# One decoder layer on one core: earlier loads of x pieces, output blocks in pairs, joined loads of keys, queries and factors

## The chip, the core and the metric

The kernel runs on one core of a Trainium2 chip. A core has a matrix engine (PE, with its weight loads listed as PEld), a vector engine (DVE), a scalar engine (ACT), GpSimd (POOL) and a sync engine (SP), which in this kernel issues every DMA. The transfers themselves are carried out by 16 DMA engines. The metric is the device time of one execution in microseconds; lower is better. The median of three runs of the kernel before is 1200.78 us (1198.64 to 1202.95).

## The reference, cut to what matters

One layer for 2048 prompt positions and 8 sample tokens, everything in float32:

```python
h = x @ w_in                       # queries, keys, values, gates of mixers A and B
for d in (1, 4, 16):               # mixer A, 8 heads: banded attention at three strides
    parts.append(band_partial(dilate(qa, d), dilate(ka, d), dilate(va, d)))
oa = merge(parts)                  # weighted by the softmax denominators
ob = merge([band_partial(qb, kb, vb)], sink)   # mixer B, 8 query heads on 2 key heads
mix = concat(oa * silu(ga), ob * silu(gb))
y = layer_norm(ALPHA * x + mix @ w_o)
```

The sample tokens go through the same layer against cached keys and values.

## The kernel before

Every float32 product is made of three products of halves: an operand is split into a rounded part and the rest (`split`: ACT copies, DVE or POOL subtracts), and the matmuls take high x high, high x low and low x high.

**Stages.** First the projections of A's keys and queries and of all keys, then the values (L527). From about 376 us on runs the attention stage, the loop at L1121 of 64 steps. A pair is two heads of one mixer. The four pairs of A have three jobs each (strides 16, 4 and 1), the four pairs of B one job; a job is four steps. A step makes the scores of one group (`scores`, L823), its weights on DVE and ACT (L831, L834), turns the weights of the step before on PE (`turn`, L853) and multiplies those of the step before that with the values (`values`, L874). In four slots of each step `advance` lets the generator `others` put work of a second stream between: the remaining projections (`stream`), then the first part of the output projection (`out_weights`). After the loop the last part computes the rest of the output projection and the layer norm (L1174).

**Order.** Inside the attention stage the order on every engine is the order in which the program is written (a manual schedule). SP issues its DMAs in that order too, and a DMA that waits holds up all that stand behind it on SP. Eight semaphores take turns for the DMAs, so a DMA also waits until the one eight places before it on SP has landed.

**The second stream (L603 to L641).** It makes three passes over x, whose split form lies in DRAM in eight chunks of 256 tokens (the last has 264), each in four pieces `gx` of 512 KB. The passes have 4, 4 and 3 column blocks of the weights (`FIRST`, then G1 to G4, then G5 to G7); one block on one chunk is 24 matmuls `pg` (L629). There are two sets of four buffers for the pieces; the pieces of the next chunk are loaded by `piece` (L576) while the present one is used.

**Keys, queries and factors.** `load_k` and `load_q` (L893, L901) fetch the keys and queries of the next pair, head by head, in halves of 1024 positions. After the last job of a pair in B, `merge_b` (L944) makes the factors of both heads, turns them on PE (`pst`, L963), writes them to DRAM (`fd`) and reads them back, spread over the 64 partitions of each head, into `F` (L976 to L981), with which the output `oT` is multiplied (L990). For A this is `merge_a` (L1001), whose loads of `F` stay as they are.

**Output blocks ahead.** The output has 17 blocks: 16 of 128 tokens and the sample tokens. For the first four, `out_weights` (L722) computes the part of the sum over the 8 row blocks of the weights (0 to 3 are A, 4 to 7 are B) that is ready: `gated` (L707) loads the gates and merged outputs of one block, `hh` and `hl` are its split form, and `out_products` (L667) does the matmuls `po`. `gated` takes 6 row blocks instead of 4 for an even block if more than one pair of B is merged by then. The last part adds what is missing (`mixed`, L648).

Of the kernel before, what the change touches and what calls it, by code (L numbers as in the profile page):

```python
# [11 lines left out]
F32 = mybir.dt.float32  # L12
F32R = mybir.dt.float32r
AF = mybir.ActivationFunctionType
OP = mybir.AluOpType
AX = mybir.AxisListType

D = 1024
# [22 lines left out]
FIRST = ["QB0", "QB1", "QB2", "G0"]  # L41
PT = (1, 4, 7, 10, 13)
RAW = 4
AHEAD = 4


def dram(t, off, ap):
# [4 lines left out]
def hymba_step(ctx, tc, xt, xs, xr, wq, wv, wo, tab, msk, ident, diag, sinks, lng, lnb,  # L52
# [513 lines left out]
    def stream(passes):  # L566

        with tc.tile_pool(name="gw", bufs=1, side="right", reuse_waits="tile") as gw, \
                tc.tile_pool(name="gx", bufs=2, side="right", reuse_waits="tile") as gx, \
                tc.tile_pool(name="go", bufs=2, side="right", reuse_waits="tile") as go, ExitStack() as fourth:  # L570
            g4 = fourth.enter_context(tc.tile_pool(name="g4", bufs=1, side="right", reuse_waits="tile"))
            news = None

            place = count(4)

            def piece(c, k0):  # L576
                c0 = 256 * c
                n = TOK - c0 if c == 7 else 256
                i = next(place) % 8
                t = (kept if i < 4 else gx).tile([128, 4 * XC], F32R, name="gx", tag="p%d" % i, bufs=1)[:, :4 * n]  # L580
                dma(t.bitcast(F32), xd[c, k0, :, :4 * n])
                t = t.rearrange("p (a k n) -> p a k n", a=2, k=2)
                return t[:, 0], t[:, 1]

            def weights(i, name):
                if i < 2:
                    t = kept.tile([128, 2, 8, 128], F32R, name="gw%d" % i, tag="w%d" % i)
                    hl = t[:, 0], t[:, 1]
                else:
                    hl = [(gw if i < 3 else g4).tile([128, 8, 128], F32R, name="gw%d%s" % (i, a)) for a in "hl"]  # L590
                ws[name].open(hl)

            ws = dict(zip(passes[0], resident_w))
            def first_wo(i):
                t = kept.tile([128, 2, 8, 128], F32R, name="wo%d" % i, tag="w%d" % i)
                wo_parts[4 + i].open((t[:, 0], t[:, 1]))

            nxt = X5
            yield 0
            for i in (2, 3):  # L600
                ws[passes[0][i]] = Parts(wq[TILES.index(passes[0][i])])
                weights(i, passes[0][i])
            for pi, names in enumerate(passes):  # L603
                more = passes[pi + 1] if pi + 1 < len(passes) else []
                if not more:
                    fourth.close()
                    sp = fourth.enter_context(tc.tile_pool(name="spb", bufs=1, side="right", reuse_waits="tile"))
                    sk = fourth.enter_context(tc.tile_pool(name="skb", bufs=1, side="right", reuse_waits="tile"))
                    news = sample("b", sp, sk)
                route = list(range(8))[::1 if pi % 2 else -1]  # L610
                for c, c2 in zip(route, route[1:] + [None]):
                    c0 = 256 * c
                    n = TOK - c0 if c == 7 else 256
                    x, nxt = nxt, []
                    if c2 is None:
                        for name in more:
                            ws[name] = Parts(wq[TILES.index(name)])
                        if not more:
                            head.append(gated(0))
                            wo_parts.update((i, Parts(wo[:, i].rearrange("p (a b) -> p a b", b=128))) for i in (4, 5))  # L620
                    for i, name in enumerate(names):
                        p = ps.tile([128, 512], F32, name="pg", tag="mm", bufs=2)
                        wh, wl = ws[name]
                        for kt in range(8):
                            if c2 is not None and kt % 2 == 0 and i == 1:
                                nxt.append(piece(c2, len(nxt)))
                            xh, xl = x[kt // 2]
                            for e, (a, b) in enumerate(((wh, xh), (wh, xl), (wl, xh))):
                                T.matmul(p[:, :n], a[:, kt, :], b[:, kt % 2, :n], start=kt + e == 0, stop=kt == 7 and e == 2)  # L629
                                yield n / 2.4  # L630
                        EMIT[name[0]](go, XC, p[:, :n], name, c0, n)
                        if name[0] == "Q":
                            queries.append(name)
                        if news:
                            next(news, None)
                        if c2 is None:
                            if not more and i < 2:
                                soon(lambda i=i: first_wo(i), 1)
                            for e in range(i, len(more) if name == names[-1] else min(i + 1, len(more))):
                                soon(lambda e=e, name=more[e]: weights(e, name), 1)  # L640
                nxt = x  # L641
            for _ in news:
                pass
# [60 lines left out]

    head = []

    def gated(tb):  # L707

        n = 6 if len(merged) > 1 and tb % 2 == 0 else 4
        cols = slice(tb * 128, tb * 128 + 128)  # L710
        t, g = [kept.tile([128, 6, 128], F32, name="h" + a, tag="p%d" % i)[:, :n] for i, a in enumerate("tg")]
        dma(g, gs[0:n, :, cols].rearrange("k p t -> p k t"))
        dma(t, ms[0:n, :, cols].rearrange("k p t -> p k t"))
        return t, g

    def late_wo(kt):
# [5 lines left out]
    def out_weights():  # L722
        wO = wscope.enter_context(tc.tile_pool(name="wO", bufs=1, side="right", reuse_waits="tile"))
        for kt in (6, 7):
            out_parts(kt, [wO.tile([128, 8, 128], F32R, name="wo%d%s" % (kt, a)) for a in "hl"])
            yield None
            yield None
        oh = wscope.enter_context(tc.tile_pool(name="oh", bufs=1, side="right", reuse_waits="tile"))
        xs_ = [oh.tile([128, D], F32, name="xh%d" % tb) for tb in range(AHEAD)]
        nxt = head[0]  # L730
        first.clear()
        for tb, x in enumerate(xs_):
            t, g = nxt
            dma(x, xr[tb * 128:tb * 128 + 128])
            for _ in range(3 if tb else 1):
                yield None
            n = t.shape[1]
            h, l = [oh.tile([128, 4, 128], F32R, name="h" + a, tag="h" + a) if tb % 2 else kept.tile([128, 6, 128], F32R, name="h" + a, tag="p%d" % (i + 2))
                    for i, a in enumerate("hl")]
            V.tensor_mul(t, t, g)  # L740
            split(h[:, :n], l[:, :n], t, V)
            yield None
            if tb + 1 < AHEAD:
                nxt = gated(tb + 1)
            for nh in range(2):
                p = ps.tile([128, 512], F32, name="po", tag="mm", bufs=2)
                yield from out_products(p, {kt: (h[:, kt], l[:, kt]) for kt in range(n)}, nh, True, True)
                xx = x[:, nh * 512:nh * 512 + 512]
                V.scalar_tensor_tensor(xx, xx, ALPHA, p, op0=OP.mult, op1=OP.add)
            first[tb] = x, n  # L750

    MI = {16: 0, 4: 1, 1: 2}
    PB, PA = (1,), (16, 4, 1)
# [139 lines left out]
    def load_k(p):  # L893
        p.k = kp.tile([128, SEQ], F32, name="k")
        for c in range(2):
            for h in range(2):
                cc = slice(1024 * c, 1024 * c + 1024)
                dma(p.k[64 * h:64 * h + 64, cc], ks[:, p.pair // 2 if p.isb else 2 + 2 * p.pair + h, cc])
            yield

    def load_q(p):  # L901
        p.q = kp.tile([128, SEQ], F32, name="q")
        for c in range(2):
            for h in range(2):
                cc = slice(1024 * c, 1024 * c + 1024)
                dma(p.q[64 * h:64 * h + 64, cc], (qb if p.isb else qa)[:, 2 * p.pair + h, cc])
            yield

    dr2 = ctx.enter_context(tc.tile_pool(name="dr2", bufs=2, space=bass.MemoryType.DRAM))
# [34 lines left out]
    def merge_b(job):  # L944
# [12 lines left out]
        V.tensor_add(dn, dn, w[:, 1])  # L957
        V.reciprocal(dn, dn)
        V.scalar_tensor_tensor(w[:, 0], w[:, 0], 0.5, dn, op0=OP.mult, op1=OP.mult)
        while where[0] < 3:  # L960
            yield
        pst = ps.tile([128, 512], F32, name="pst", tag="pt", bufs=2)
# [13 lines left out]
        def fetch(c):  # L976
            F = at.tile([128, 768], F32, name="F", bufs=2)
            n = min(768, SEQ - 768 * c)
            for a in range(2):
                dma(F[a * 64:a * 64 + 64, :n], dram(fd, a * SEQ + c * 768, [[0, 64], [1, n]]))  # L980
            Fs.append(F[:, :n])  # L981

        fetch(0)
# [355 lines left out]
```

## Time and profile before

| | before |
|---|---|
| profiled execution, time | 1196.65 us |
| profiled execution, span | 1194.9 us |
| median of 3 runs | 1200.78 us |
| DMA issues by SP | 1011 |
| matmuls in the attention stage and the rest, up to the sample block | 376 to 1026 us |
| last part, from the sample block on | 1026 to 1195 us |

The profile's page gives the busy time of each engine, the span in slices, the DMA queues and the costliest groups of instructions; further views give the busy time and the DMA share by stretches of time ("windows"), who waited for whom ("waits"), and the instructions in order of time ("timeline"). "DMA share" is the mean busy share of the 16 DMA engines. PEclk is the share of full speed at which the matrix engine's clock was granted.

### The profile page before, as it was taken

Reading aid. Unit: us, or ns where it says so; the run is one execution under the profiler, and the core shown is the slowest. Engines: PE = TensorE matmul, PEld = TensorE weight load, DVE = VectorE, ACT = ScalarE, POOL = GpSimd, SP = SyncE. Lnnn points to the kernel's source line nnn. Section 1 sums busy time; section 2 is a strip of 40 time slices with the busy share of each in tenths; the row PEclk is TensorE's granted clock in tenths of the full one; section 3 lists DMA queues with packets and bytes.
Section 4 is the critical chain, followed back from the end, with each engine's and each line's share of the span. In section 5 each row is a group of like instructions: output and inputs, shape, how many; then the busy total and the mean of one; then the engine's idle time right before and its main releaser. Section 6 shows DMA issues by size and latency. Waiting matters only on the chain.

```text
span 1194.9 us, 23402 instructions
## 1 busy us (share of the span) xinstructions
PE 1138.3 (95%) x8614; PEld 1004.4 (84%) x8614; DVE 540.0 (45%) x1787; ACT 438.1 (37%) x1417; POOL 360.0 (30%) x470
## 2 busy tenths in 40 slices
PE   8999999999989999999998999998999997999997
PEld 7899999988978988997887879887878875688885
DVE  6532000011002455565565546554656664675534
ACT  3200011111102556565565545554555451232211
POOL 2243010220002200034704401462254534275532
PEclk9999999999999999999999999998999998999998
DMA  8845888375495575458677856866897967555531
GB/s 275 267 132 160 255 269 281 106 227 177 150 316 172 181 185 164 133 129 216 194 207 166 210 174 158 208 157 201 198 237 190 305 191 214 172 190 181 179 107 70
DMA packets 206066, 230.14 MB, mean 193 GB/s; under 512 B 34640, under 2 KB 174576, under 8 KB 205568
## 3 DMA queue, kind: packets, MB, share of 16 engines
q1 hardware_dynamic: 205952, 228.66, 66.3%
q8 instruction: 67, 1.10, 0.4%
q14 instruction: 47, 0.39, 0.1%
HBM read 158.52 MB, written 70.07 MB: 191 GB/s over the span
## 4 chain that ended last, share of the span: by engine, by line
PE 68%; DMA 17%; POOL 4%; issue 3%; DVE 3%; ACT 3%; SPq 2%; POOLq 0%; DVEq 0%; ACTq 0%
PE po L672 13%; PE pg L629 12%; PE pv L527 7%; PE ps_s L823 6%; PE ps_o L874 6%; DMA F<-fd 5%; PE ps_pt L853 5%; PE ppt L152 5%; PE pmm L152 5%; PE ps L152 5%; PE po L152 3%; DMA gx<-xd 3%; DMA wvf<-in_wv 1%; ACT pe L834 1%; DMA fd<-wts 1%
## 5 line engine op out<-in xcount | busy, mean ns | idle before, releaser
L834 ACT ACTIVATE pe<-sm,st 128x256 f32<-128x256 f32 (+1 forms) x512 | 236.6, 464 | 218.0 <-DVE st L831 217.4
L831 DVE CUSTOM_DVE_ANT_0 sm<-ps_s,mk 128x256 f32<-128x256 f32 (+1 forms) x512 | 180.2, 375 | 193.0 <-PE ps_s L823 129.4
L629 PE MATMUL pg<-gx,gw 128*128 128x256 f32 (+1 forms) x1104 | 169.0, 295 | 18.5 <-DMA gx<-xd 13.6
L629 PEld LDWEIGHTS pg<-gx,gw 128*128 128x128 f32 x1104 | 143.0, 192 | 21.4 <-DMA gx<-xd 15.3
L853 PE MATMUL ps_pt<-idt,pe 128*128 128x128 f32 x848 | 134.5, 279 | 1.9 <-DVE pT L859 1.4
L1050 POOL TENSOR_TENSOR oT<-oT,F 128x256 f32<-128x256 f32 x32 | 23.7, 742 | 339.5 <-DMA F<-fd 302.2
L859 DVE COPY pT<-ps_pt 128x512 f32<-128x512 f32 x176 | 120.6, 685 | 5.5 <-PE ps_pt L853 5.0
L853 PEld LDWEIGHTS ps_pt<-idt,pe 128*128 128x128 f32 x848 | 96.1, 141 | 15.5 <-issue 8.8
L874 PE MATMUL ps_o<-pT,v 128*64 128x128 f32 (+1 forms) x1120 | 107.1, 335 | 0.0
L874 PEld LDWEIGHTS ps_o<-pT,v 128*64 128x64 f32 x1120 | 70.2, 137 | 40.1 <-issue 16.6
L834 ACT ACTIVATION_READ_ACCUMULATOR pe<-sm,st 128x1 f32 x512 | 96.5, 188 | 0.0
L823 PE MATMUL ps_s<-k,qo 64*128 64x256 f32 (+1 forms) x768 | 94.4, 387 | 0.0
L823 PEld LDWEIGHTS ps_s<-k,qo 64*128 64x128 f32 x768 | 68.5, 193 | 13.2 <-issue 1.7
L629 PE MATMUL pg<-gx,gw2h 128*128 128x256 f32 (+1 forms) x368 | 75.7, 293 | 1.8 <-ACT spe L406 1.8
L527 PE MATMUL pv<-wvh,xl 128*128 128x384 f32 (+1 forms) x224 | 69.9, 312 | 0.0
L527 PE MATMUL pv<-wvh,xh 128*128 128x384 f32 (+1 forms) x224 | 69.8, 312 | 0.0
L527 PE MATMUL pv<-wvl,xh 128*128 128x384 f32 (+1 forms) x224 | 69.7, 311 | 0.0
L629 PEld LDWEIGHTS pg<-gx,gw2h 128*128 128x128 f32 x368 | 58.6, 191 | 2.1 <-ACT spe L406 2.1
L672 PE MATMUL po<-wl,mho 128*128 128x512 f32 x192 | 59.8, 393 | 0.0
L539 ACT ACTIVATE vf<-pv 128x384 f32<-128x384 f32 (+1 forms) x32 | 14.0, 437 | 113.0 <-PE pv L527 63.7
L629 PE MATMUL pg<-gx,gw2l 128*128 128x256 f32 (+1 forms) x184 | 54.3, 295 | 0.2 <-POOL gw2l L138 0.2
L260 POOL TENSOR_TENSOR wl<-w,wh 128x512 fp32r<-128x512 f32 x18 | 24.5, 1374 | 83.9 <-DVE wh L259 62.9
(262 smaller groups left out, 2474.7 us busy)
## 6 DMA issues: line engine op xcount, KB each, us to landing
gx<-xd SPq DMA_DIRECT2D x80, 512.0 KB
F<-fd SPq DMA_DIRECT2D x80, 192.0 KB
gs<-th SPq DMA_DIRECT2D x64, 128.0 KB
v<-vs SPq DMA_DIRECT2D x28, 256.0 KB
xd<-xh SPq DMA_DIRECT2D x12, 512.0 KB
xd<-xl SPq DMA_DIRECT2D x12, 512.0 KB
kc<-in_kca SPq DMA_DIRECT2D x8, 768.0 KB
vc<-in_vca SPq DMA_DIRECT2D x6, 1024.0 KB
```

The costliest lines, as they stand in the source:

```text
L152: T.matmul(p[:, :n], a[:, kt, :], b, start=k == 0, stop=k == 23)
L260: (V if between else G).tensor_sub(l[:, k0:k0 + 4], w, h[:, k0:k0 + 4].bitcast(F32))
L527: T.matmul(p[:, :w], l, r[:, kt, :w], start=k == 0, stop=k == 23)
L629: T.matmul(p[:, :n], a[:, kt, :], b[:, kt % 2, :n], start=kt + e == 0, stop=kt == 7 and e == 2)
L672: T.matmul(p, a, b[:, nh * 4:nh * 4 + 4].rearrange("p a b -> p (a b)"), start=first and k == 0, stop=last and k == end)
L823: T.matmul(s[:, h, n % 4, :w], self.Q[g][r, n % 4 * 128:n % 4 * 128 + 128], self.keys(n)[r], start=True, stop=True)
L831: V.tensor_tensor_reduce(sm[:, :w], self.s[:, h, n % 4, :w], mk[:, MI[self.d], 256 - w:], -0.125, 3.0e38, op0=OP.add, op1=OP.min, accum_out=m)
L834: S.activation(p[:, :w], sm[:, :w], AF.Exp, scale=-1.0, bias=m, accum_out=den)
L853: T.transpose(pt[:, h, j], self.P[h, n][:, a:a + 128], idt)
L859: V.tensor_copy(t, pt)
L874: T.matmul(o[64 * h:64 * h + 64, a:a + 128 * len(ns)], v[:, cv, kv:kv + 64], t[:, h, j:j + len(ns)].rearrange("p a b -> p (a b)"), start=n ...
L1050: G.tensor_mul(m, m, F[:, 0])
```

## The change

Four edits, here in the diff cut to its core:

```diff
-                            if c2 is not None and kt % 2 == 0 and i == 1:
+                            if c2 is not None and (i, kt) in ((0, 2), (0, 4), (0, 6), (1, 0)):
                                 nxt.append(piece(c2, len(nxt)))
...
-    def gated(tb):
-        n = 6 if len(merged) > 1 and tb % 2 == 0 else 4
-        cols = slice(tb * 128, tb * 128 + 128)
-        t, g = [kept.tile([128, 6, 128], F32, name="h" + a, tag="p%d" % i)[:, :n] for i, a in enumerate("tg")]
+    def gated(j):
+        cols = slice(j * 256, j * 256 + 256)
+        t, g = [kept.tile([128, 4, 256], F32, name="h" + a, tag="p%d" % i) for i, a in enumerate("tg")]
...
-        for tb, x in enumerate(xs_):
+        for j in range(2):
             t, g = nxt
+            xs_ = [(oh if tb < 3 else kp).tile([128, D], F32, name="xh%d" % tb, ...) for tb in (2 * j, 2 * j + 1)]
+            for tb, x in zip((2 * j, 2 * j + 1), xs_):
+                dma(x, xr[tb * 128:tb * 128 + 128])
...
     def load_k(p):
         for c in range(2):
-            for h in range(2):
-                cc = slice(1024 * c, 1024 * c + 1024)
-                dma(p.k[64 * h:64 * h + 64, cc], ks[:, p.pair // 2 if p.isb else 2 + 2 * p.pair + h, cc])
+            h = p.pair // 2 if p.isb else 2 + 2 * p.pair
+            dma(p.k[:, 1024 * c:1024 * c + 1024], dram(ks, h * TOK + 1024 * c, [[0 if p.isb else TOK, 2], [10 * TOK, 64], [1, 1024]]))
     def load_q(p):
...
+            dma(p.q[:, 1024 * c:1024 * c + 1024], dram(qb if p.isb else qa, 2 * p.pair * TOK + 1024 * c, [[TOK, 2], [8 * TOK, 64], [1, 1024]]))
...
         V.scalar_tensor_tensor(w[:, 0], w[:, 0], 0.5, dn, op0=OP.mult, op1=OP.mult)
+        yield
         while where[0] < 3:
             yield
         pst = ps.tile([128, 512], F32, name="pst", tag="pt", bufs=2)
...
-            for a in range(2):
-                dma(F[a * 64:a * 64 + 64, :n], dram(fd, a * SEQ + c * 768, [[0, 64], [1, n]]))
+            dma(F[:, :n], dram(fd, c * 768, [[SEQ, 2], [0, 64], [1, n]]))
```

A joined load has 128 partitions on the chip's side, and on the DRAM side a pattern of three dimensions whose outermost has 2 entries, the heads. The output blocks ahead are done two at a time, with 4 row blocks for all four.

The rows below, and those in the two fences after them, are the program's order on one engine, without any time. On SP, in the attention stage while the third pair's keys are fetched (`k<-ks`), among the factors of A (`F<-fd`), pieces of x (`gx`), merged outputs (`ms`) and gates (`gs`), before:

```order
L1038 DMA F<-fd_5260 64x3x256 x2
L898 DMA k<-ks 64x1024 x2
L581 DMA gx<-xd 128x1024 x2
L1058 DMA ms<-oT_5524 128x256
L898 DMA k<-ks 64x1024 x2
L581 DMA gx<-xd 128x1024
L1038 DMA F<-fd_5260 64x3x256 x2
L581 DMA gx<-xd 128x1024
```

The same place after the change:

```order
L580 DMA gx<-xd 128x1024
L1036 DMA F<-fd_5258 64x3x256 x2
L580 DMA gx<-xd 128x1024
L1056 DMA ms<-oT_5522 128x256
L580 DMA gx<-xd 128x1024
L174 DMA gs<-th 128x256
L1036 DMA F<-fd_5258 64x3x256 x2
L898 DMA k<-ks 128x1x1024
L580 DMA gx<-xd 128x1024
L1056 DMA ms<-oT_5522 128x256
L898 DMA k<-ks 128x1x1024
L1036 DMA F<-fd_5258 64x3x256 x2
```

Three of the four pieces now stand ahead of the keys, the fourth between the two halves; each half of the keys is one DMA of 128 partitions instead of two of 64.

On PE, around the last but one turn of factors (`pst`), between turns of weights (`ps_pt`) and gate matmuls (`pg`), before:

```order
L853 MATMUL ps_pt<-idt,pe 128x128 x4
L629 MATMUL pg<-gx,gw_9611 128x256 x8
L963 MATMUL pst<-idt,wts 32x128
L823 MATMUL ps_s<-k,qo 128x256 x8
L874 MATMUL ps_o<-pT,v 64x256 x6
```

And after:

```order
L854 MATMUL ps_pt<-idt,pe 128x128 x4
L628 MATMUL pg<-gx,gw_9595 128x256 x8
L962 MATMUL pst<-idt,wts 32x128
L824 MATMUL ps_s<-k,qo 128x256 x8
L875 MATMUL ps_o<-pT,v 64x256 x6
```

Nothing moved here: the chain of factors takes one slot more on paper, but it waits for the step's last slot in either version. This holds for all four turns of factors.

On SP, where the factors of B's second pair are read back, before (`hg`, `ht` are the loads of `gated`):

```order
L968 DMA fd_10612<-stT 16x16x8 x2
L581 DMA gx<-xd 128x1024 x3
L980 DMA F<-fd_10612 64x768 x4
L581 DMA gx<-xd 128x1024
L175 DMA gs<-th 128x256 x2
L980 DMA F<-fd_10612 64x512 x2
L712 DMA hg<-gs 128x4x128
L713 DMA ht<-ms 128x4x128
```

And after:

```order
L580 DMA gx<-xd 128x1024 x3
L174 DMA gs<-th 128x256
L967 DMA fd_10596<-stT 16x16x8 x2
L580 DMA gx<-xd 128x1024
L978 DMA F<-fd_10596 128x1x768 x2
L174 DMA gs<-th 128x256 x2
L978 DMA F<-fd_10596 128x1x512
L710 DMA hg<-gs 128x4x256
L711 DMA ht<-ms 128x4x256
```

Six loads of factors became three, and the first loads for the output blocks are twice as large.

More of the change, by code (lines that the diff above doesn't have):

```diff
@@ L43 @@
 RAW = 4
-AHEAD = 4
 def dram(t, off, ap):
@@ L705, in hymba_step @@
     head = []
-    def gated(tb):
-        n = 6 if len(merged) > 1 and tb % 2 == 0 else 4
-        cols = slice(tb * 128, tb * 128 + 128)
-        t, g = [kept.tile([128, 6, 128], F32, name="h" + a, tag="p%d" % i)[:, :n] for i, a in enumerate("tg")]
-        dma(g, gs[0:n, :, cols].rearrange("k p t -> p k t"))
-        dma(t, ms[0:n, :, cols].rearrange("k p t -> p k t"))
+    def gated(j):
+        cols = slice(j * 256, j * 256 + 256)
+        t, g = [kept.tile([128, 4, 256], F32, name="h" + a, tag="p%d" % i) for i, a in enumerate("tg")]
+        dma(g, gs[0:4, :, cols].rearrange("k p t -> p k t"))
+        dma(t, ms[0:4, :, cols].rearrange("k p t -> p k t"))
         return t, g
@@ L728, in out_weights @@
         oh = wscope.enter_context(tc.tile_pool(name="oh", bufs=1, side="right", reuse_waits="tile"))
-        xs_ = [oh.tile([128, D], F32, name="xh%d" % tb) for tb in range(AHEAD)]
         nxt = head[0]
         first.clear()
-        for tb, x in enumerate(xs_):
+        for j in range(2):
             t, g = nxt
-            dma(x, xr[tb * 128:tb * 128 + 128])
-            for _ in range(3 if tb else 1):
+            xs_ = [(oh if tb < 3 else kp).tile([128, D], F32, name="xh%d" % tb, **(dict(tag="k", bufs=2) if tb == 3 else {}))
+                   for tb in (2 * j, 2 * j + 1)]
+            for tb, x in zip((2 * j, 2 * j + 1), xs_):
+                dma(x, xr[tb * 128:tb * 128 + 128])
+            for _ in range(1 if j == 0 else 2):
                 yield None
-            n = t.shape[1]
-            h, l = [oh.tile([128, 4, 128], F32R, name="h" + a, tag="h" + a) if tb % 2 else kept.tile([128, 6, 128], F32R, name="h" + a, tag="p%d" % (i + 2))
+            h, l = [oh.tile([128, 4, 256], F32R, name="h" + a) if j else kept.tile([128, 4, 256], F32R, name="h" + a, tag="p%d" % (i + 2))
                     for i, a in enumerate("hl")]
             V.tensor_mul(t, t, g)
-            split(h[:, :n], l[:, :n], t, V)
+            split(h, l, t, V)
             yield None
[L743 to L750, printed above, removed]
+            if j == 0:
+                nxt = gated(1)
+            for tb, x in zip((2 * j, 2 * j + 1), xs_):
+                cols = slice(tb % 2 * 128, tb % 2 * 128 + 128)
+                for nh in range(2):
+                    p = ps.tile([128, 512], F32, name="po", tag="mm", bufs=2)
+                    yield from out_products(p, {kt: (h[:, kt, cols], l[:, kt, cols]) for kt in range(4)}, nh, True, True)
+                    xx = x[:, nh * 512:nh * 512 + 512]
+                    V.scalar_tensor_tensor(xx, xx, ALPHA, p, op0=OP.mult, op1=OP.add)
+                first[tb] = x, 4
     MI = {16: 0, 4: 1, 1: 2}
@@ L903, in load_q @@
         for c in range(2):
-            for h in range(2):
-                cc = slice(1024 * c, 1024 * c + 1024)
-                dma(p.q[64 * h:64 * h + 64, cc], (qb if p.isb else qa)[:, 2 * p.pair + h, cc])
+            dma(p.q[:, 1024 * c:1024 * c + 1024], dram(qb if p.isb else qa, 2 * p.pair * TOK + 1024 * c, [[TOK, 2], [8 * TOK, 64], [1, 1024]]))
             yield
```

## The prediction

> **What bounds the kernel now.** I read the page's busy times first, then the chain, then the stages.
>
> ```profile
> PE 1138.3 (95%) x8614; PEld 1004.4 (84%) x8614; DVE 540.0 (45%) x1787; ACT 438.1 (37%) x1417; POOL 360.0 (30%) x470
> ```
>
> ```profile
> PE 68%; DMA 17%; POOL 4%; issue 3%; DVE 3%; ACT 3%; SPq 2%; POOLq 0%; DVEq 0%; ACTq 0%
> ```
>
> The first line gives each engine's busy time (us, share of the span, instructions), the second the chain that ended last, by engine. PE is busy 95% of the span, so no wait that is left is large; the second thing on the chain is the transfers. What they could do is seen by stages. The windows are the four pairs of A, and then the rest of the attention stage with B's pairs and the start of what follows:
>
> ```profile
> core 0: us, PE busy (x), PEclk, DMA share, GB/s
> 376.00:484.00 108.00, 105.18 (x951) 0.98 0.61 183
> 484.00:592.00 108.00, 106.33 (x965) 0.98 0.65 162
> 592.00:702.00 110.00, 102.22 (x890) 0.95 0.79 212
> 702.00:819.00 117.00, 112.72 (x1017) 1.00 0.64 154
> 819.00:855.00 36.00, 33.46 (x268) 0.91 0.81 223
> 855.00:895.00 40.00, 36.64 (x328) 0.96 0.94 224
> 895.00:933.00 38.00, 35.16 (x306) 1.00 0.80 207
> 933.00:969.00 36.00, 33.55 (x298) 1.00 0.77 253
> 969.00:1006.00 37.00, 29.95 (x202) 0.93 0.73 226
> ```
>
> In each row the numbers behind the stretch are its length, the busy time of PE, the granted clock, the mean busy share of the 16 DMA engines and the bytes moved. PE sets the pace everywhere, but from 819 us on the DMA engines are at 0.73 to 0.94. A change that spreads the same bytes less evenly has room for little there.
>
> The waits that the change aims at are those for pieces of x:
>
> ```profile
> PE pg L629 <- DMA gx<-xd: 13.6, 7, 4.1
> PE pst L963 <- DVE wts L959: 4.6, 2, 2.4
> ```
>
> (total, times, longest). The 13.6 us have a second price, which the timeline and the windows at the same places show:
>
> ```profile
> 658.59 1.65 PE L629 MATMUL pg<-gx,gw 128*128 128x256 f32 x6 [3.94 <-DMA gx<-xd]
> 692.17 0.50 PE L629 MATMUL pg<-gx,gw 128*128 128x256 f32 x2 [1.68 <-DMA gx<-xd]
> 821.42 2.12 PE L629 MATMUL pg<-gx,gw 128*128 128x256 f32 x7 [4.05 <-DMA gx<-xd]
> ```
>
> ```profile
> 550.10:553.50 3.40, 3.40 (x20) 0.50 0.95 247
> 655.90:662.70 6.80, 4.11 (x20) 0.50 0.91 247
> 693.50:696.90 3.40, 3.40 (x20) 0.50 0.95 314
> 819.70:826.60 6.90, 5.18 (x22) 0.51 0.96 331
> ```
>
> Around each wait the clock was granted at a half, for 20.5 us in all; had PE worked through at full clock, 10.3 us of it would be gained. The Trainium skill, "TensorE: Matmul & The Clock Gate", section "HAM oscillation — how this bites in real kernels", advises to leave no idle gap over about 3.4 us. The trace is stricter here, since the 1.68 us gap at 692 also had its half clock.
>
> **The change part by part.** *Pieces a step ahead.* They are issued 18 matmuls earlier, about half a step (108 us are twelve steps of 9), in the order of SP only; PE, DVE and ACT keep their order. If the transfers keep their pace, that covers all seven waits: the longest, 4.05, is shorter than the 5 us won. Worth up to 13.6 + 10.3 = 24 us.
>
> *The later turn of factors* moves no matmul: the four `pst` stay between the same neighbours on PE, so the 4.6 us of the row above stay. 0, and certain from the order alone.
>
> *Output blocks in pairs.* Each block's products wait for its split:
>
> ```profile
> 992.01 0.71 PE L672 MATMUL po<-wl,hh 128*128 128x512 f32 x2 [1.31 <-ACT hh L109]
> 1001.30 1.22 PE L672 MATMUL po<-wl,hh 128*128 128x512 f32 x2 [3.12 <-ACT hh L109]
> 1011.76 1.20 PE L672 MATMUL po<-wl,hh 128*128 128x512 f32 x4 [1.80 <-ACT hh L109]
> ```
>
> ```profile
> 1000.70:1007.50 6.80, 6.20 (x15) 0.50 1.03 268
> 991.24 0.62 ACT L109 ACTIVATE hh<-ht 128x512 fp32r<-128x512 f32 x1
> 1010.87 0.84 ACT L109 ACTIVATE hh<-ht 128x768 fp32r<-128x768 f32 x1 [9.62 <-DVE ht L740]
> ```
>
> The two later waits go (3.12 + 1.80), with them half of the 6.8 us at half clock (3.4): 8.3. Splits of 128x1024 have no row; by the 0.62 and 0.84 us of 512 and 768 elements one takes about 1.06, and with its subtraction and the wait of the first pair on it I take 2.3 of the 8.3 back, between 0 and 6: some 6 us won. Twelve `po` matmuls move from this place to the last part and cost the same there.
>
> *The joined loads* decide. Their issues become fewer:
>
> ```profile
> k<-ks SPq DMA_DIRECT2D x20, 256.0 KB
> q<-qb SPq DMA_DIRECT2D x16, 256.0 KB
> q<-qa SPq DMA_DIRECT2D x12, 256.0 KB
> F<-fd SPq DMA_DIRECT2D x8, 128.0 KB
> 898.43 5.96 SPq L463 DMA_DIRECT2D od<-vsd  x8
> ```
>
> 38 issues go (10 + 14 of keys and queries, 14 of factors). One takes 0.6 us of SP (2.37 us for four factors, in a row further down), so 23 us, and nobody waits for SP in these stages: 0. But a joined load reads its source as 2 x 64 x n, with the heads outermost, where a load of one head had 64 outermost. One load of before has this form: the eight in the last row, mixer B's sample outputs, with a source whose outermost dimension is 2. The trace's semaphore records, which no view prints, show how it runs: the count comes up in three steps, a jump at 1.0 us and then two single ones (at 1.72 and 1.75, or 3.65 and 3.99 us after the issue). The same load for mixer A, with 8 outermost, has a jump and eight single steps, and a load with 128 outermost 16 single ones. I read a single step as one DMA engine that is done: two engines do the work where 2 is outermost. The Trainium skill, "DMA: Bandwidth & Descriptors", section "Why a DMA increments its semaphore by 16 and not by 1", says it in a rule: the number of engines is the largest up to 16 that divides the slowest dimension of both patterns, and they are the lowest-numbered ones. The trace agrees on the number; which engines they are it doesn't show.
>
> What two engines cost comes from the busiest stretch, 698 to 702 us, in which all 16 were taken:
>
> ```profile
> DMA packets 449, 1.64 MB, mean 411 GB/s; under 512 B 48, under 2 KB 48, under 8 KB 449
> q1 hardware_dynamic: 449, 1.64, 101.6%
> ```
>
> 411 / (16 x 1.016) = 25.3 GB/s for one engine. Half of a pair's keys or queries is 512 KB, 262 KB on each of two engines: 10.4 us, where it was 1.3 us on each of 16. So these two get 9.1 us more for each half, 18 for a pair's keys and 18 for its queries. A load of factors with 768 columns (384 KB) adds 6.8 and one of 512 adds 4.5: 13.6 and 4.5 for a pair's two and one in the first and last group, 18 in all. Every other load has a sixteenth of its bytes on these engines too, in order behind the joined ones. Whoever needs a piece of x needs it from all engines, so the two set the pace once they have more work than a stage is long.
>
> Their work in a stage is its length x DMA share, and the joined loads that it issues. A's pairs have keys and queries, 36:
> - 108 x 0.61 + 36 = 102, 108 x 0.65 + 36 = 106, 110 x 0.79 + 36 = 123, 117 x 0.64 + 36 = 111 us.
> - B: 36 x 0.81 + 18 = 47; 40 x 0.94 + 36 = 74; 38 x 0.80 + 32 (queries and factors) = 62; 36 x 0.77 + 23 (factors) = 51; 37 x 0.73 + 36 (two pairs' factors) = 63. That is 297 us in stages that are 187 long.
>
> No engine is busy all the time; the best stage above has 0.94, so I divide by it. A: 108.5, 113, 131 and 118 against 108, 108, 110 and 117, or 0.5 + 5 + 21 + 1 = 27 more. B: 297 / 0.94 = 316, 129 more. Together **+156**. The gains on pieces, and those of the output blocks, lie beside this wait and count nothing: PE waits for these engines anyway. Two things I set against each other. The last pair's factors have cover before the last part needs what they make:
>
> ```profile
> 1000.06 2.37 SPq L980 DMA_DIRECT2D F<-fd  x4
> 1011.26 0.69 DVE L990 TENSOR_TENSOR oT<-oT,F 128x512 f32<-128x512 f32 x1
> 1035.08 0.39 PE L672 MATMUL po<-wo6h,mlp 128*128 128x512 f32 x1
> ```
>
> The last multiplication starts at 1011.3, and the first product with its result at 1035.1: 24 us. Against that, two halves in a row (20.8 us) use up all the lead that a piece behind them has:
>
> ```profile
> 404.68 0.87 SPq L581 DMA_DIRECT2D gx<-xd  x2
> 419.38 0.28 PE L629 MATMUL pg<-gx,gw 128*128 128x256 f32 x1
> ```
>
> 14.7 us before, some 20 with the change; a clump on a queue that is late already has no cover.
>
> **Bounds.** If the two engines never idle and all of the cover counts, the sum is 123 (13 in A's third pair, 110 in B) - 24 = +99. Lower still if a packet's time has waiting in it: weighed by bytes, B's other loads are 223, 224, 207, 253 and 226 GB/s of 411, or 103 us in place of 152, B has 103 + 145 = 248 us in 187, and no stage of A overflows: +61. Upwards: in the stage with 253 GB/s at 0.77 a busy engine moves 253 / (16 x 0.77) = 20.5 GB/s; a half then takes 12.8 us, and the 290 us of joined work grow by 23%, 67 us, +71 by 0.94: +227. With an engine idle somewhat more often than in the best stage it is a little over that; I go to +255.
>
> **The rivals.**
> - *The change does what it says*: the joined loads are spread over 16 engines. For it: the chip's side of the load has 128 partitions, as the pieces of x have. Against: the od loads have 8 partitions, and two steps. Then -13.6 - 10.3 - 6 = -30: 1196.65 - 30 = 1167 us. It decides from eight engines on: a half then adds 2.6 - 1.3 = 1.3 us in place of 9.1, B's joined work 21 us in place of 145, and 152 + 21 stays below 187. The rule of the Trainium skill's DMA page, above, speaks against this one; without it the sum is this 1167, with it the 1353 below.
> - *Two engines, but other ones from load to load*: then each engine has one eighth of the joined work on average, no stage overflows, and only a load's own 10 us counts; a half ordered 13 us before its pair begins (queries at 798 to 801, needed at 810) is late by some 10 us, others are in time. -30 + 10 + some 13 for pieces behind a half, as much as they wait now: about 1190.
> - *Nothing moves*: the pieces' waits are replaced by as much waiting behind clumps; 1197.
>
> **How the numbers follow.** The profiled execution was at 1196.65 us, 1.75 more than its span of 1194.9, and 0.3% below the median of three, 1200.78; a difference of 0.3% is about what can be told from none. Forecast: 1196.65 + 156 = **1353 us**, chance 0.84 for a slowdown by two busy engines at any price; 0.08 for 1167, 0.05 for 1190, 0.03 for no change. Faster 0.12 (part of the 1190 case lies within 0.3%), same 0.04, slower 0.84. The range for 8 in 10 is that of the likeliest case: from +61 to +255, **1258 to 1452**. It leaves out the rivals.
>
> **What the profile of the changed kernel would show.** If right: joined loads that take 10 us and more from issue to landing; a DMA share that falls in B's stages while PE waits; waits of PE for `gx` in place of 13.6 us over 100; the attention stage ends after 1080 us, and three quarters of the added time lie behind 819 us. The `pst` waits are unchanged. If wrong: an attention stage that still ends near 990 us, `gx` waits near 0, and a joined load that lands as fast as a piece of x. A stage of A that grows as much as one of B would show that the sum by load is wrong, though not the two engines.

## The result, and the profile after

The changed kernel takes 1391.26 us, median of four runs (1387.93 to 1394.75), against 1201.23 us before: the ratio is 1.158, with a 95% interval of 1.154 to 1.163. The forecast was 1353 us with a range of 1258 to 1452. The profiled execution has a span of 1385.9 us, 191.0 more than before. The page of after, busy times and chain:

```profile
PE 1168.5 (84%) x8614; PEld 1028.2 (74%) x8614; DVE 550.3 (40%) x1784; ACT 438.8 (32%) x1416; POOL 360.8 (26%) x471
...
PE 50%; DMA 35%; POOL 4%; SPq 4%; issue 2%; DVE 2%; ACT 2%; POOLq 0%; DVEq 0%; ACTq 0%
```

The matmuls are the same 8614, but their busy time has grown by 30 us: by the trace's clock records the matrix engine had 215 us at half clock, where it had 46 before. The transfers' share of the chain that ended last has doubled, from 17% to 35%. The windows of after follow the pairs, four of A and four of B (length, PE busy, clock, DMA share, GB/s):

```profile
core 0: us, PE busy (x), PEclk, DMA share, GB/s
380.60:491.20 110.60, 103.58 (x914) 0.97 0.53 155
491.20:624.60 133.40, 110.05 (x944) 0.91 0.52 140
624.60:753.60 129.00, 107.02 (x942) 0.92 0.64 171
753.60:886.60 133.00, 109.61 (x938) 0.91 0.50 142
886.60:943.20 56.60, 41.93 (x334) 0.85 0.64 180
943.20:1015.40 72.20, 44.16 (x369) 0.79 0.44 119
1015.40:1093.30 77.90, 43.16 (x338) 0.78 0.45 134
```

The kernel now waits for transfers, and yet the 16 DMA engines are less busy than before: 0.44 in B's second pair, where the nearest window of before had 0.94. A mean over 16 engines falls like this when a few are overloaded and the others idle; that it is a few shows below. The waits of PE after (total, times, longest), and those of DVE for factors:

```profile
PE ps_pt L854 <- ACT oT L892: 47.3, 5, 30.9
PE sob L444 <- DMA vc<-in_vcb: 24.6, 2, 24.4
PE ps_pt L854 <- DVE pT L860: 20.6, 5, 11.2
PE pg L628 <- POOL gw L136: 15.5, 2, 9.8
...
PE pg L628 <- DMA gx<-xd: 5.4, 4, 3.9
PE pst L962 <- DVE wts L957: 2.1, 2, 1.1
```

```profile
DVE oT L988 <- DMA F<-fd: 75.8, 6, 34.7
```

PE hardly waits for pieces of x. It waits for ACT and DVE, which wait for loads. The chain shows how the longest of these waits comes about (start, time, what):

```profile
1050.30 33.02 DMA F<-fd
1083.33 0.02 issue
1083.35 0.03 DVE oT L988
...
1084.23 0.41 DVE th L171
1084.64 0.34 DVE sm L832
...
1085.02 1.09 ACT pe L835 x4
1086.11 0.49 ACT oT L892
```

A joined load of factors takes 33 us from the start of its issue to its landing. DVE stands at the multiplication with it (L988), and behind that on DVE stand the weights of the next step, behind these on ACT the evacuation `oT` (L892) that frees the bank for PE's next turns. In the window of this wait PE does nothing at all, and its clock is down:

```profile
1060.70:1086.60 25.90, 0.00 (x0) 0.50 0.37 116
```

Where the 191 us are, in lengths from one pair's first scores to the next's, up to the sample block, and after it (worked out from the starts of the matmuls of both traces; the first row is the start):

| | before | after | more |
|---|---|---|---|
| start of A's first pair | 378.9 | 380.6 | 1.7 |
| A, pairs 1 to 4 | 104.1, 105.8, 115.4, 105.8 | 110.6, 133.3, 129.1, 132.9 | 74.8 |
| B, pairs 1 to 3 | 44.9, 45.5, 42.7 | 56.6, 72.1, 77.9 | 73.5 |
| B's pair 4 and blocks ahead | 82.9 | 120.8 | 37.9 |
| from the sample block on | 168.8 | 171.8 | 3.0 |

That two engines are late shows in the semaphore records, which no view prints. The chain has a half of B's keys, then a piece of x, then the sample's cached values (`vc`):

```profile
944.41 26.64 DMA k<-ks
973.02 17.20 DMA gx<-xd
990.24 16.49 DMA vc<-in_vcb
```

The joined keys count up in a jump and two steps, as the loads `od` did before. They had landed when the piece was issued; the joined load ahead of the piece is the first half of the queries, issued at 972.40 and landed at 988.96. Of the piece, 14 engines are done between 5.5 and 7.2 us after the issue, and two at 16.9 and 17.2. Where two joined loads of factors were issued 0.6 us apart with nothing ahead of them, the first landed 10.4 us after its issue and the second 17.7 after its own, or 7.9 us after the first. In all four pairs of B the second of two such loads landed 7.9 to 9.1 us after the first. One waits for the other, so they are on the same two engines.

```profile
1178.66 10.39 DMA F<-fd
```

SP is held up too. From 370 us on, 60 of its issues took over 1.5 us each, 249 us together; before there were 14, with 29 us. Two of the long stretches (start, time, count last):

```profile
459.06 12.67 SPq L580 DMA_DIRECT2D gx<-xd  x1
1049.75 13.23 SPq L978 DMA_DIRECT2D F<-fd  x2
```

The first comes right after two halves of joined queries (456.00 and 458.36), the second is two joined loads of factors. SP issues in order, so whatever stands behind such an issue starts late. Without joined loads (the first run below) there are 16 such issues with 32 us.

### The profile page after: what moved, and what is told of

Its sections match the earlier page's. It is cut to its first block, busy times and chain, and to the rows that moved or that the text cites. A ratio compares the mean times of both kernels' runs of the same rounds, so it can differ in the third digit from the quotient of the medians.

```text
span 1385.9 us, 23352 instructions
## 1 busy us (share of the span) xinstructions
PE 1168.5 (84%) x8614; PEld 1028.2 (74%) x8614; DVE 550.3 (40%) x1784; ACT 438.8 (32%) x1416; POOL 360.8 (26%) x471
## 4 chain that ended last, share of the span: by engine, by line
PE 50%; DMA 35%; POOL 4%; SPq 4%; issue 2%; DVE 2%; ACT 2%; POOLq 0%; DVEq 0%; ACTq 0%
DMA F<-fd 12%; PE po L671 11%; PE pg L628 8%; PE pv L526 6%; DMA gx<-xd 4%; PE ps L151 4%; PE pmm L151 4%; PE ppt L151 4%; PE ps_s L824 3%; PE ps_o L875 3%; PE ps_pt L854 3%; DMA raw<-in_wo 2%; PE po L151 2%; DMA k<-ks 2%; DMA xh<-in_xr 2%
## 5 line engine op out<-in xcount | busy, mean ns | idle before, releaser
L854 PE MATMUL ps_pt<-idt,pe 128*128 128x128 f32 x848 | 141.8, 290 | 76.4 <-ACT oT L892 47.3
L628 PE MATMUL pg<-gx,gw 128*128 128x256 f32 (+1 forms) x1104 | 178.3, 305 | 25.0 <-POOL gw L136 15.5
L628 PEld LDWEIGHTS pg<-gx,gw 128*128 128x128 f32 x1104 | 151.6, 202 | 28.4 <-POOL gw L136 16.1
L854 PEld LDWEIGHTS ps_pt<-idt,pe 128*128 128x128 f32 x848 | 100.9, 147 | 91.2 <-ACT oT L892 48.7
L875 PE MATMUL ps_o<-pT,v 128*64 128x128 f32 (+1 forms) x1120 | 110.8, 343 | 22.5 <-DVE pT L860 13.8
L171 DVE SCALAR_TENSOR_TENSOR th<-th,pg 128x256 f32<-128x256 f32 (+1 forms) x64 | 26.9, 420 | 81.3 <-ACT th L167 80.8
```

The lines of the kernel that those rows point to most:

```text
L171: V.scalar_tensor_tensor(th[:, :n], th[:, :n], 1.0, p, op0=OP.add, op1=OP.mult)
L854: T.transpose(pt[:, h, j], self.P[h, n][:, a:a + 128], idt)
L875: T.matmul(o[64 * h:64 * h + 64, a:a + 128 * len(ns)], v[:, cv, kv:kv + 64], t[:, h, j:j + len(ns)].rearrange("p a b -> p (a b)"), start=n ...
```

## The experiments

All times are medians beside runs of the kernel before on the same chip (1199 to 1203 us). Of the kernels below, those with joined loads and the one with loads of 62 rows were run twice each.

**1. Which part of the change costs it.** The joined loads were undone in the changed kernel, all of them, and then one kind at a time; and they were made alone in the kernel before. The edit, for queries (keys and factors alike):

```diff
-            dma(p.q[:, 1024 * c:1024 * c + 1024], dram(qb if p.isb else qa, 2 * p.pair * TOK + 1024 * c, [[TOK, 2], [8 * TOK, 64], [1, 1024]]))
+            for h in range(2):
+                cc = slice(1024 * c, 1024 * c + 1024)
+                dma(p.q[64 * h:64 * h + 64, cc], (qb if p.isb else qa)[:, 2 * p.pair + h, cc])
```

Without joined loads:

> The changed kernel with its keys, queries and factors loaded head by head again; earlier pieces, pairs and the later turn stay. Theory A (joined loads run on the same two DMA engines): the loss goes altogether and the gains of the other edits show, 1167 us, 1160 to 1190; waits of PE for pieces near 0. Theory B (the pieces that now stand ahead of keys, queries and factors push those back): still near 1390 us. Theory C (the blocks in pairs, which now wait for larger loads, lose the time): also near 1390.

1187.47 us, ratio 0.986 (0.980 to 0.992): theory A, and the waits for pieces are gone:

```profile
PE pg L628 <- DMA gx<-xd: 0.8, 3, 0.4
```

The joined loads cost 1391 - 1187 = 204 us; B and C fall. Joined loads alone:

> The kernel before with the joined loads alone. Theory A: 1385 to 1425 us, as slow as the changed kernel or a little slower, since the earlier pieces have no cover to add there; factors of 768 columns take 10 us and more from issue to landing. Theory B: 1200 us or some us less (38 issues fewer). Theory C: 1200 us.

1406.1 us, ratio 1.169 (1.160 to 1.178): theory A. Here, without the earlier pieces, the waits have the form that the prediction had named:

```profile
PE pg L629 <- DMA gx<-xd: 73.3, 16, 12.2
```

In the changed kernel these 73.3 us are down to 5.4, but the time is only 15 us shorter (1406 against 1391; the two intervals overlap a little). The pieces come earlier, and PE waits elsewhere: for `oT` 47.3 us in place of 32.4, for `pT` on DVE (`ps_pt`) 20.6 in place of 1.1. Keys and queries joined, then factors:

> The changed kernel with factors loaded head by head, keys and queries still joined. Theory A: A's pairs as long as in the changed kernel (506 us together, 431 before), B's stages over by 11 + 34 + 10 by the sums of the prediction: some 130 over the version without joined loads, about 1300 us. Theory B: near 1390.

> The changed kernel with keys and queries loaded head by head, factors of B still joined. Theory A: A's pairs as before (431 us together), the loss only from B's second pair on, 50 to 75 us over the version without joined loads, 1220 to 1240. With the run of joined keys and queries the two losses add up to about that of all joined loads, or less where one covers the other. Theory B: near 1390.

1338.07 us (ratio 1.112, 1.102 to 1.122) and 1244.66 us (1.035, 1.027 to 1.043), that is 151 and 57 over 1187: 208 together, where all joined loads cost 204. For keys and queries that is more than was expected (some 130, about 1300 us); for factors it is as expected. The two losses add up, within intervals of about 10 us each way, and they lie where each kind is loaded. A's four pairs take 505 us with joined keys and queries, and 422 with joined factors, as without any (420).

**2. What it is in a joined load.** The divisor of its outermost dimension, or the form? In the kernel before, each load of one head's keys or queries was cut in two, by rows:

```diff
-                dma(p.k[64 * h:64 * h + 64, cc], ks[:, p.pair // 2 if p.isb else 2 + 2 * p.pair + h, cc])
+                for r0, r1 in ((0, 62), (62, 64)):
+                    dma(p.k[64 * h + r0:64 * h + r1, cc], ks[r0:r1, p.pair // 2 if p.isb else 2 + 2 * p.pair + h, cc])
```

> The kernel before; each load of one head's keys or queries (64 rows) is cut into one of 62 rows and one of 2. Nothing is joined, the bytes are the same, 48 issues are added. Theory A in the form of the divisor rule (62 and 2 go on two engines each): joined keys and queries cost 151 us in the changed kernel, so about 1350 us, 1320 to 1380. Theory D (what costs is the joined form itself: a pattern with one dimension more, or a single large load for both heads): 1201 to 1215.

> The same with 60 rows and 4, which by the divisor rule go on 15 and on 4 engines. Theory A: 1200 to 1215 us, as many issues as with 62 and 2 notwithstanding. Theory E (added issues, or uneven loads of any kind, cost it): about what 62 and 2 rows give.

1360.27 us (ratio 1.129, 1.121 to 1.138) with 62 and 2 rows, 1205.82 (1.003, 1.001 to 1.006) with 60 and 4. Nothing is joined in either, and both have the same bytes and issues. In the semaphore records a load of 62 rows has a jump and two steps (the last mostly 9 to 19 us after the issue), one of 60 rows a jump and 15. So D falls, and E too: the number of engines decides. The other way round, a joined load on 16 engines:

> The changed kernel with keys and factors head by head, queries alone joined: 14 of the 24 joined halves of keys and queries. Theory A: 14/24 of 151 us over 1187, about 1275 us, 1240 to 1290.

> The same with the queries joined in as many loads of the same size, but kept head by head in DRAM, so that the two heads are 128 rows in one dimension (the stores of the queries become 16 x 8 rows). Theory A: the joined loads run on 16 engines and the time is that without joined loads, 1187 us, 1178 to 1195. Theory D, if a large load for both heads is what costs: as the run of joined queries, about 1275.

```diff
-    qa = dr.tile([64, 8, TOK], F32, name="qa")
+    qa = dr.tile([8, 64, TOK], F32, name="qa").rearrange("h d t -> d h t")
...
-            dma(p.q[:, 1024 * c:1024 * c + 1024], dram(qb if p.isb else qa, 2 * p.pair * TOK + 1024 * c, [[TOK, 2], [8 * TOK, 64], [1, 1024]]))
+            dma(p.q[:, 1024 * c:1024 * c + 1024], dram(qb if p.isb else qa, 2 * p.pair * 64 * TOK + 1024 * c, [[TOK, 128], [1, 1024]]))
```

1281.53 us (ratio 1.064, 1.055 to 1.073) on two engines, 1188.93 (0.987, 0.979 to 0.995) on 16. The load has the same size and the same place in the program; its source has 128 outermost instead of 2, and the loss of 94 us over 1187 is gone.

**3. The other edits alone.** The kernel before with the earlier pieces, with the pairs, and both without the later turn:

```diff
-                            if c2 is not None and kt % 2 == 0 and i == 1:
+                            if c2 is not None and (i, kt) in ((0, 2), (0, 4), (0, 6), (1, 0)):
```

> The kernel before with the earlier pieces alone. By the prediction's step 24 us less: 1177. But without joined loads all edits together gave only 14 us, though the waits of PE for pieces fell from 13.6 to under 1 us; so either the half clock costs less than 10.3 us (then about 1188 us here, and pairs and later turn are worth nothing), or this edit gives its 24 (1177) and another one takes 10 back (then the kernel without the later turn or the one without pairs shows it).

> The kernel before with the blocks in pairs alone, all four blocks with 4 row blocks. By the prediction's step 6 us less: 1195 to 1196. If the pairs take back what the pieces win: 1206 to 1212.

> Earlier pieces and pairs, without the later turn and without joined loads. If the later turn moves nothing that matters: the same as with it, 1187 us, 1182 to 1192. If it takes something back (the waits of PE for the turn of factors were 7.0 us in the run without joined loads, 4.6 before): some 3 to 10 us less.

1188.97 us (ratio 0.990, 0.986 to 0.994), 1196.28 (0.995, 0.992 to 0.998) and 1190.24 (0.990, 0.987 to 0.993). The pairs give 6.3 us, the later turn nothing that these runs can tell (1190.24 without it, 1187.47 with it). The pieces give 13.6, not 24. Their waits went, and others became longer; the waits of PE in that run, of which those of the first row were 6.2 before, and those of the second not there:

```profile
PE po L672 <- ACT hh L109: 7.6, 3, 4.3
...
PE ps_pt L853 <- ACT oT L891: 4.5, 2, 3.0
...
PE pg L629 <- DMA gx<-xd: 2.5, 3, 1.5
```

By the clock records of that run the time at half clock between 370 and 1010 us fell by 13.6 us, from 34.1 to 20.5; the prediction had four stretches of 20.5 us go and none come. Both gains together should be 20 us and are 12 to 14; the intervals, 3 to 7 us each way, leave open whether part of one gain is lost beside the other.

**4. Why A lost more than the sum said.** With joined keys and queries, the four halves of a pair of A were issued one by one, at steps 3, 5, 7 and 9 of a pair, in place of two by two at 5 and 8:

```diff
-        loads[s0 + (0 if before.isb else 5)] = p, "k"
-        loads[s0 + (1 if before.isb else 8)] = p, "q"
+        if before.isb:
+            loads[s0] = p, "k"
+            loads[s0 + 1] = p, "q"
+        else:
+            for e, (c, what) in zip((3, 5, 7, 9), ((0, "k"), (1, "k"), (0, "q"), (1, "q"))):
+                loads[s0 + e] = p, what + str(c)
```

> The kernel of joined keys and queries (1338 us), with the four halves of a pair of A issued one by one, two steps apart, instead of two by two; the same loads, bytes and number of issues. The prediction's sum had A's second to fourth pairs 27 us over, by the mean work of the two engines in a stage; they are some 25 us over each. Theory F (what counts is the clump: two halves in a row hold up for 20 us what stands behind them, the factors of A's pair before among it): each of these three pairs 10 to 15 us shorter, 1295 to 1310 us. Theory G (the two engines are short of time over the whole pair, wherever the halves stand): within 10 us of 1338.

1322.18 us, 16 less than 1338 and between both expectations; but the intervals overlap (1.095 to 1.111 against 1.103 to 1.122), and the two profiled executions are 9 us apart. Of the windows of A's pairs

```profile
379.80:486.40 106.60, 101.79 (x914) 0.98 0.60 174
486.40:606.80 120.40, 108.25 (x941) 0.93 0.57 143
606.80:741.00 134.20, 110.60 (x942) 0.89 0.61 167
741.00:873.80 132.80, 107.85 (x937) 0.93 0.55 153
```

the second is 12.6 us shorter than with halves two by two (133.0, and 133.4 in the changed kernel), as theory F has it, and the third and fourth are not (129.9 and 132.9). So the clump counts in one pair, by one profile of this kernel, and theory F fails for the other two. The time that SP spends in its DMA issues moves along with this: 59 us in the second pair in place of 75, but 74 and 69 in the third and fourth in place of 77 and 75. No run shows whether that is what holds these two up.

## Why the prediction held, and where it did not

- **Two engines for a joined load: shown.** The number by the semaphore records and by the pair of 62 and 60 rows; that two loads share the same two, by the factors that landed one after the other in each pair of B. Which of the 16 they are is not shown. The Trainium skill's rule on the number of engines ("DMA: Bandwidth & Descriptors"), weighed in the prediction, held in each of the four forms that were run: 2 heads, 62, 60 and 128 rows gave 2, 2, 15 and 16 counted steps.
- **The price of a load: right.** At the prediction's 25.3 GB/s for one engine, half of a load of 768 columns takes 7.8 us; the second of two landed 17.7 + 0.6 - 10.4 = 7.9 us after the first.
- **The sum: right in sign and about in size, +156 against +190; the terms were off.** That the total is nearer than its terms is partly luck, since one term was too small and another too large. A's pairs were to lose 27 us and lost 75. The step "their work in a stage is its length x DMA share, and the joined loads that it issues" lets any idle time of a stage take any load of it. In A's first pair, which loads joined keys and queries but has no factors of an earlier pair to wait for, the loss is 6.5 us; in each later one 14 to 28. The prediction's own sign of a wrong sum by load was there: A's second pair grew by 27.5 us, B's second by 26.6. B, with what follows up to the sample block, was to lose 129 and lost 111. What makes A's later pairs lose so much stays open in part (experiment 4).
- **The lower clock was no term.** The sum counted PE's waits and not what they do to PE: 30 us more busy time for the same matmuls. How much of it lengthens the time, and how much would have been waited anyway, no run shows.
- **SP was put at nothing.** "Nobody waits for SP in these stages: 0" was worked out from 38 issues fewer, but the issues took longer (249 us in place of 29, above). No run shows how much of the loss comes by this way.
- **The place of the waits: wrong.** "Waits of PE for `gx` in place of 13.6 us over 100": they are 5.4. I took the reader of the late piece for the one that would wait, but pieces were given a lead by the same change; without that lead the waits are 73.3 us, still under 100. Engines whose loads had less lead stopped first, and PE behind them: DVE at the factors of B (75.8 us, 6.0 before), POOL at the same (62.2, 24.5 before) and at the weights. "Three quarters of the added time behind 819 us" fails with it: when B begins, 76 of 191 us are already lost.
- **What else it said**: the `pst` waits are no larger (2.1 us, 4.6 before), the attention stage ends after 1080 us, and the DMA share falls in B's stages, as it said.
- **The gains under the loss.** "Count nothing" did not hold: the other edits give 14 us without joined loads (1201 to 1187) and some 15 with them (1406 to 1391, 12 us either way). The rival that does what the change says was priced at 1167 us; without joined loads it is 1187. The step that failed is "13.6 + 10.3 = 24 us". Part of it was counted twice: in the four windows at half clock PE was busy for 16.1 of the 20.5 us, so half clock cost at most 8.0, and the idle rest is already in the 13.6. And of the 13.6 us of waits 11.1 went, but other waits and other stretches at half clock came. The pairs' 6 us were right.

## What to carry to other kernels

Before two loads are joined, look at the outermost dimension of both sides of the joined one: where it was 2 here, two DMA engines carried all of the load, and a transfer over 16 engines issued behind it waited for its part on these two (17 us, where the other 14 engines were done after 7). Such a queue shows as late loads and long issues beside a *falling* mean DMA share, and PE's own wait list may name it nowhere. If loads are to be joined, lay the data in DRAM so that the 128 rows are one dimension (here 94 us between the two layouts of one scratch tensor); the change without its joined loads takes 1187 us, and the runs cannot tell it from the earlier pieces alone (1189).

## What the runs showed that was not expected

- The Trainium skill, "DMA: Bandwidth & Descriptors", section "Rules for kernel authors", advises one transfer of 128 partitions in place of two for the halves; the same section also says that an outermost dimension under 16 confines a DMA to that many engines at most. Joining all three kinds of loads with two heads outermost follows the first and breaks the second, and costs 204 us of 1391. Joining the queries alone with 128 rows in one dimension follows both (1188.93 against 1187.47 us), and neither a cost nor a gain can be told.
- 48 more issues and uneven loads of 60 and 4 rows cost next to nothing (1205.82 us, ratio 1.003), although the four-row loads run on four engines only.
- Loads alone can hold PE still for long: with joined loads it waited 24.4 us at once for the sample's cached values, which lie in another tensor that the change doesn't touch. In the chain above the second of their two loads starts when the late piece has landed, and takes 16.5 us itself; 14 of its engines were done after 6.5.
